# Layer 0 of a diffusion backbone: mean and Newton step of the inverse roots of queries and keys on GpSimd in place of VectorE

## The chip, the cores and the metric

One NeuronCore of a Trainium2 chip. It has a matrix engine (TensorE, PE below; its weight loads are PEld), VectorE (DVE), ScalarE (ACT), GpSimd (POOL) and SyncE (SP), which issues most DMAs. Each engine works through its own list of instructions in order, and waits on semaphores for the others. The metric is the device time of one execution in microseconds (us).

## The reference

Two layers of a backbone over 1024 latent tokens with a prefix of 256 context tokens, width 1024, float32. Layer 0 (the even layer) runs two kinds of grouped-query attention beside each other, each with 8 query heads and 2 key heads of width 64: [A] global, with RMSNorm of every query and key head and a rotary step, and [B] windowed, with a sink logit. Layer 1 runs a conformer convolution and a two-dimensional neighbourhood attention. The change lies in [A]'s RMSNorm:

```python
def rms_norm(x, g):
    xf = x.astype(jnp.float32)
    y = xf * lax.rsqrt(jnp.mean(xf * xf, axis=-1, keepdims=True) + EPS)
    return (y * g.astype(jnp.float32)).astype(x.dtype)
...
    def project(h):
        aq, ak, av, ag, bq, bk, bv, bg = split_cols(h @ w_in, EVEN_WIDTHS)
        aq = rms_norm(heads(aq, A_HEADS), q_gain)
        ak = rms_norm(heads(ak, A_KV_HEADS), k_gain)
...
    aq, ak, bq, bk = (apply_rope(t, cos, sin) for t in (aq, ak, bq, bk))
...
    y_lat = jnp.concatenate([oa * jax.nn.silu(ag), ob * jax.nn.silu(bg)], axis=-1) @ w_out
```

## The kernel before

The 1280 tokens are ten blocks of 128. Layer 0 treats four key heads `u` one after the other, in the order 2, 3, 0, 1: u = 2 and 3 are the windowed heads, u = 0 and 1 the global ones with the RMSNorm. A float32 matmul is made of three: every operand is split into a rounded part (on ACT, line 308: `hh`, `wh`, `hc`, `ph`) and a residual (on POOL or DVE, line 311: `hl`, `wl`, `hc`, `pl`), and PE multiplies high by high, low by high and high by low (lines 328 to 330).

Two strands are woven. The main one is attention for the head whose keys are ready, over blocks of 128 queries and chunks of 128 keys. It first finds upper bounds of the scores: PE computes them into the tile `mx` (lines 616, 628, 636), which has two banks, and DVE reduces them to `mp` (618, 629, 637 with a mask). DVE then makes the negated maximum `nmt` (412, or 415 to 422 with the sink), PE transposes it (`trn`, 433), and DVE puts it into `QL` (434), which enters the scores `st` (505, 509). ACT takes the exponent (`pf`, 517) and its rounded part `ph`; POOL subtracts to get the residual `pl` (in the blocks meant here DVE takes only every twelfth); PE multiplies by the values (`ov`, 456 to 461); DVE finishes the block (466 to 469, 666, 668).

The other strand fills in: it projects the next head (`proj_qkv`) and then its gate (`proj_gate`, product `pg`). `proj_qkv` makes five passes over pairs of token blocks. Each pass has two times 24 matmuls into the bank `pq`, which ACT copies to `pc` (three buffers, [128 tokens, 2 blocks, 5 heads of 64 and one of values]). For u = 0 and 1, and so ten times in all, the group of this change follows: ACT squares `pc` (line 844), DVE sums each head to `ss` (847, 128x10), makes the mean (848), POOL raises it to the power -0.5 (242, in `newton_rsqrt`), DVE refines it by one Newton step (243 to 245), and multiplies `pc` by the result `nr` (850) and by the gain (852). Then come the rotary products on DVE (861, 863) and their addition on POOL (865), and at last `qk_tail`: PE transposes the pair (`trk`, 873), ACT and DVE split it into `qs` and into the keys `KAt`, and SP writes `qs` to DRAM (876), from where attention loads it. Groups 0 to 4 below are those of u = 0 (305 to 370 us), groups 5 to 9 those of u = 1 (435 to 525 us). Lines 854 and 855 split the values into `Vt`. `newton_rsqrt` is called elsewhere too, from `rstd_steps` among others.

No order is written out by hand. A scheduler takes the program's instructions, simulates a timeline from its own cost estimates, and fixes each engine's list from it; priorities (`later`) and `issue_after` marks steer it. A changed instruction can thus shift the order of the instructions around it, on every engine.

## Time and profile before

| | |
|---|---|
| median of 3 runs | 1565.03 us (1564.26 to 1565.88) |
| the profiled execution | 1565.51 us, span 1563.7 us |
| mean granted TensorE clock | 0.963 |
| span in 21480 instructions: PE / DVE / ACT / POOL busy | 1465.1 / 1049.0 / 747.2 / 799.8 us |
| the ten powers (line 242, 128x10) on POOL | 19.6 us, 1963 ns each |

The span is the profiled time from the first to the last instruction. "Busy" leaves out waits, and a busy share averages over stages in which other engines set the pace. In a row of the timeline the first number is the start in us, the second the duration; then come engine, line, operation, output and inputs with their shapes, and in brackets how long the engine had been idle ahead of it and which instruction released it. A clock of 1.00 in a stretch means that PE ran at full speed there.

### The profile page before, as it was taken

To read this page: it belongs to the slowest core of one execution; us is meant where nothing else is said; L and a number is where in the kernel's file an instruction comes from. 1 tells how busy PE (TensorE), PEld (TensorE's weight loads), DVE (VectorE), ACT (ScalarE), POOL (GpSimd) and SP (SyncE) were. 2 spreads that over 40 slices of the span, in tenths; PEclk is the share of its full clock that TensorE was granted. 3 is DMA by queue.
4 is the path that set the end of the run, shared out by engine and by line. 5 is a ranking of instruction groups with operands and counts; after the bars stand their busy time and mean duration, and the time that the engine had idled before them with its cause. 6 is when DMAs were issued, how large, how long until landed. Compare 5 with 4: busy or idle time off the path is not lost.

```text
span 1563.7 us, 21480 instructions
## 1 busy us (share of the span) xinstructions
PE 1465.1 (94%) x7084; PEld 1174.2 (75%) x7084; DVE 1049.0 (67%) x2113; ACT 747.2 (48%) x1418; POOL 799.8 (51%) x637
## 2 busy tenths in 40 slices
PE   6899999998998999999999878999999999889995
PEld 2786887896896768876767557888887888667875
DVE  2832556589579765466677956999756466776766
ACT  3721434444435565447556663443334355554563
POOL 3430434455445766557646663665632244454665
PEclk7899999999999999999999989999999999889997
DMA  9473315422312245121112012111445788967632
GB/s 365 151 246 129 102 61 182 142 69 92 118 51 78 93 155 172 54 68 49 51 31 86 13 34 85 59 55 41 141 159 195 214 243 250 277 179 214 187 110 108
DMA packets 154168, 199.83 MB, mean 128 GB/s; under 512 B 14716, under 2 KB 95816, under 8 KB 154056
## 3 DMA queue, kind: packets, MB, share of 16 engines
q1 hardware_dynamic: 147392, 186.88, 38.0%
q10 hardware_dynamic: 6664, 11.57, 2.3%
q8 instruction: 56, 0.92, 0.3%
q14 instruction: 56, 0.46, 0.1%
HBM read 148.07 MB, written 49.02 MB: 126 GB/s over the span
## 4 chain that ended last, share of the span: by engine, by line
PE 73%; DVE 15%; DMA 4%; issue 3%; POOL 3%; ACT 2%; SPq 0%; DVEq 0%; ACTq 0%; POOLq 0%
PE p L328 6%; PE p L330 6%; PE p L329 6%; PE po L328 4%; PE po L329 4%; PE po L330 4%; PE ov L456 4%; PE ov L458 4%; PE ov L457 4%; PE st L505 3%; PE st L509 3%; PE pq L328 2%; PE pq L329 2%; PE pq L330 2%; PE pg L328 2%
## 5 line engine op out<-in xcount | busy, mean ns | idle before, releaser
L311 POOL TENSOR_TENSOR pl<-pf,ph 128x512 fp32r<-128x512 f32 (+4 forms) x321 | 394.8, 1241 | 359.7 <-ACT ph L308 305.8
L517 ACT ACTIVATE pf<-st 128x512 f32<-128x512 f32 x284 | 166.1, 596 | 204.3 <-PE st L509 164.3
L311 POOL TENSOR_TENSOR wl<-wr,wh 128x512 fp32r<-128x512 f32 (+2 forms) x131 | 170.5, 1314 | 164.6 <-ACT wh L308 137.7
L308 ACT CAST ph<-pf 128x512 fp32r<-128x512 f32 (+4 forms) x364 | 208.9, 587 | 26.9 <-PE ov L457 17.0
L328 PE MATMUL p<-hh,wh 128*128 128x512 f32 x448 | 178.0, 398 | 5.5 <-ACT hh L308 2.8
L329 PE MATMUL p<-hl,wh 128*128 128x512 f32 x448 | 176.2, 394 | 0.6 <-POOL hl L311 0.6
L330 PE MATMUL p<-hh,wl 128*128 128x512 f32 x448 | 173.8, 394 | 0.0
L456 PE MATMUL ov<-ph,Vt 128*128 128x512 f32 (+4 forms) x364 | 143.4, 394 | 8.3 <-DVE y L666 4.6
L505 PE MATMUL st<-QH,KAt 128*128 128x512 f32 (+4 forms) x364 | 141.4, 389 | 8.6 <-ACT pf L517 7.8
L458 PE MATMUL ov<-pl,Vt 128*128 128x512 f32 (+4 forms) x364 | 142.3, 391 | 2.0 <-POOL pl L311 1.9
L457 PE MATMUL ov<-ph,Vt 128*64 128x512 f32 (+4 forms) x364 | 140.4, 386 | 0.0
L509 PE MATMUL st<-QL,KBt 68*128 68x512 f32 (+4 forms) x364 | 136.0, 384 | 0.9 <-DVE QL L434 0.8
L1079 DVE SCALAR_TENSOR_TENSOR cps<-U,taps,cps 128x512 f32<-128x512 f32 x184 | 126.3, 748 | 0.9
L308 ACT CAST wh<-wr 128x512 fp32r<-128x512 f32 (+2 forms) x134 | 81.1, 613 | 91.8 <-DMA wr<-in_od_d_dram 19.9
L328 PEld LDWEIGHTS p<-hh,wh 128*128 128x128 f32 x448 | 85.3, 190 | 24.2 <-ACT hh L308 3.0
L329 PEld LDWEIGHTS p<-hl,wh 128*128 128x128 f32 x448 | 85.0, 190 | 19.1 <-POOL hl L311 1.7
L330 PEld LDWEIGHTS p<-hh,wl 128*128 128x128 f32 x448 | 85.1, 190 | 17.5
L629 DVE TENSOR_REDUCE mp<-mx 128x1 f32<-128x512 f32 x128 | 85.1, 680 | 17.8 <-PE mx L628 16.8
L328 PE MATMUL pq<-wh,hh 128*128 128x384 f32 x256 | 88.1, 344 | 2.8 <-ACT hh L308 2.8
L505 PEld LDWEIGHTS st<-QH,KAt 128*128 128x128 f32 x364 | 69.5, 191 | 27.5 <-ACT pf L517 12.1
L948 DVE SCALAR_TENSOR_TENSOR x<-po,modT,x 128x512 f32<-128x512 f32 (+1 forms) x72 | 47.0, 656 | 64.2 <-PE po L330 63.7
L456 PEld LDWEIGHTS ov<-ph,Vt 128*128 128x128 f32 x364 | 71.2, 196 | 24.9 <-ACT ph L308 5.2
(280 smaller groups left out, 3492.6 us busy)
## 6 DMA issues: line engine op xcount, KB each, us to landing
mw<-in_mod_w_dram SPq DMA_DIRECT2D x16, 1024.0 KB, 5.5
Q<-qs SPq DMA_DIRECT2D x40, 256.0 KB, 2.2
QH<-Q SPq DMA_DIRECT2D x80, 128.0 KB, 2.7
mw<-in_mod_w_dram SPq DMA_DIRECT2D x16, 512.0 KB, 6.5
wr<-in_od_d_dram SPq DMA_DIRECT2D x32, 256.0 KB, 3.1
wr<-in_ev_qkv_dram SPq DMA_DIRECT2D x16, 384.0 KB, 5.3
KAt<-KD SPq DMA_DIRECT2D x16, 384.0 KB, 6.2
wr<-in_od_wo_dram SPq DMA_DIRECT2D x22, 256.0 KB, 3.4
```

The source lines that it names most:

```text
L308: acts.append(SC.copy(hi, src))
L311: (GP if leng == "g" else VE).tensor_tensor(lo, src, hi.bitcast(F32), op=ALU.subtract)
L328: PE.matmul(o, lh, rh, start=first, stop=False)
L329: PE.matmul(o, lh, rl, start=False, stop=False)
L330: PE.matmul(o, ll, rh, start=False, stop=last)
L456: PE.matmul(o, V[:, 64:192], ph[:, :n], start=(t == 0), stop=False)
L457: PE.matmul(g.ov[0:64, q0 : q0 + n], V[:, 0:64], ph[:, :n], start=False, stop=False)
L458: PE.matmul(o, V[:, 64:192], pl[:, :n], start=False, stop=(last and g.sink is None))
L505: sts.append(PE.matmul(st[:, :n], KA[:, cs], g.QH[:, q0 : q0 + n], start=True, stop=False))
L509: PE.matmul(st[:, :n], KB[0:68, cs], g.QL[0:68, q0 : q0 + n], start=False, stop=True)
L517: acts.append(SC.activation(pf[:, :n], st[:, :n], AF.Exp, scale=1.0 if g.bias else SCALE))
L1079: VE.scalar_tensor_tensor(pc, uc, w, pc, op0=ALU.mult, op1=ALU.add)
```

## The change

In the groups of u = 0 and 1 the mean (848) and the three instructions of the Newton step, so far on DVE, become POOL instructions. The third DVE instruction form (a product with a constant folded in) is taken apart, so the Newton step has four instructions instead of three. DVE loses four instructions in each of ten groups; POOL has six where it had one. DVE hands `ss` over one instruction earlier and gets `nr` back finished.

```diff
--- before.py
+++ after.py
@@ -845,8 +845,14 @@
                     ss = ap.tile([P, 16], F32, tag="ss", name=nm("ss"), bufs=2)
                     s10 = ss[:, 0:10].rearrange("p (j h) -> p j h", j=2)
                     VE.tensor_reduce(s10, t2, axis=AX.X, op=ALU.add)
-                    VE.tensor_scalar(ss[:, 0:10], ss[:, 0:10], 1.0 / 64.0, EPS, op0=ALU.mult, op1=ALU.add)
-                    r = newton_rsqrt(ap, ss[:, 0:10], 10, "sr")
+                    GP.tensor_scalar(ss[:, 0:10], ss[:, 0:10], 1.0 / 64.0, EPS, op0=ALU.mult, op1=ALU.add)
+                    r = ap.tile([P, 16], F32, tag="srr", name=nm("nr"), bufs=2)
+                    t = ap.tile([P, 16], F32, tag="srt", name=nm("nt"), bufs=2)[:, 0:10]
+                    GP.tensor_tensor(r[:, 0:10], ss[:, 0:10], mhalf[:, 0:10], op=ALU.pow)
+                    GP.tensor_tensor(t, r[:, 0:10], r[:, 0:10], op=ALU.mult)
+                    GP.tensor_tensor(t, t, ss[:, 0:10], op=ALU.mult)
+                    GP.tensor_scalar(t, t, -0.5, 1.5, op0=ALU.mult, op1=ALU.add)
+                    GP.tensor_tensor(r[:, 0:10], r[:, 0:10], t, op=ALU.mult)
                     VE.tensor_tensor(p5, p5, r[:, 0:10].rearrange("p (j h) -> p j h", j=2)[:, :, :, None]
                                      .broadcast_to([P, 2, 5, 64]), op=ALU.mult)
                     VE.tensor_tensor(p5, p5, gain5[:, None, :, :].broadcast_to([P, 2, 5, 64]), op=ALU.mult)
```

From line 856 of the new kernel on, a line has a number higher by six: the product of `pc` and `nr`, 850 before, is 856, the gain 858, the addition on POOL 871. The number of instructions on PE, ACT and SP stays as it was but for a pair of rows on PE that are counted together. The scheduler's order is the same on all engines up to some 305 us, differs to about 850 us, is the same on PE from there to about 1350 us, and differs once more on PE and SP to about 1395 to 1420 us. In the rows below, a name's number is that of its buffer, and runs on differently in the two programs: `pc_3599`, `ss_3813`, `nr_3816` of before are `pc_3602`, `ss_3816`, `nr_3819` now (group 3), and `pc_5854`, `nr_6095` are `pc_5863`, `nr_6104` (group 9).

DVE in group 3, before (from the product of `pc` with `nr` to the sink block's `nmt`):

```order
L850 TENSOR_TENSOR pc_3599<-pc_3599,nr_3816 128x2x320
L637 ISA mx_2837,mp_2819<-mx_2837,k_bm 128x384
L637 ISA mp_2819 128x1
L852 TENSOR_TENSOR pc_3599<-pc_3599,gain_529 128x2x320
L861 TENSOR_TENSOR rt_852_3811<-pc_3599,k_cs 128x320 x2
L637 ISA mx_2852,mp_2819<-mx_2852,k_bm 128x384
L637 ISA mp_2819 128x1
L311 TENSOR_TENSOR qs_3887<-trk_3883,qs_3887 128x256
L863 TENSOR_TENSOR pc_3599<-pc_3599,k_cs 128x2x320
L415 TENSOR_REDUCE m_624_2856<-mp_2819 128x4
L311 TENSOR_TENSOR KAt_543<-trk_3883,KAt_543 64x128
L417 TENSOR_TENSOR nmt_2855<-m_624_2856,sink_155 128x4
```

DVE at the same place now:

```order
L637 ISA mx_2852,mp_2819<-mx_2852,k_bm 128x384
L637 ISA mp_2819 128x1
L311 TENSOR_TENSOR qs_3891<-trk_3887,qs_3891 128x256
L415 TENSOR_REDUCE m_624_2856<-mp_2819 128x4
L417 TENSOR_TENSOR nmt_2855<-m_624_2856,sink_155 128x4
L419 SCALAR_TENSOR_TENSOR se_2859<-nmt_2855,sink 128x4
L311 TENSOR_TENSOR KAt_543<-trk_3887,KAt_543 64x128
L421 CAST nmt_2855<-se_2859 128x4
L422 TENSOR_TENSOR nmt_2855<-se_2859,nmt_2855 128x4
L856 TENSOR_TENSOR pc_3602<-pc_3602,nr_3819 128x2x320
L466 STREAM_TRANSPOSE r_721_3263<-ov_3142 64x256 x2
L858 TENSOR_TENSOR pc_3602<-pc_3602,gain_529 128x2x320
```

The whole chain of `nmt` (415 to 422), which stood behind the products of `pc`, now stands ahead of them; the Newton step's three rows are gone.

POOL in group 3, before, from a split ahead of the power on:

```order
L311 TENSOR_TENSOR pl_2899<-pf_2900,ph_2898 128x512
L242 TENSOR_TENSOR nr_3816<-ss_3813,mhalf 128x10
L311 TENSOR_TENSOR pl_2919<-pf_2920,ph_2918 128x512
L311 TENSOR_TENSOR pl_3036<-pf_3037,ph_3035 128x512
L311 TENSOR_TENSOR wl_4005<-wr_4003,wh_4004 128x512
L311 TENSOR_TENSOR pl_3117<-pf_3118,ph_3116 128x512
L311 TENSOR_TENSOR wl_4011<-wr_4009,wh_4010 128x512
L865 TENSOR_TENSOR pc_3599<-pc_3599,rt_852_3811 128x2x320
```

POOL at the same place now:

```order
L848 TENSOR_SCALAR ss_3816<-ss_3816 128x10
L311 TENSOR_TENSOR pl_2919<-pf_2920,ph_2918 128x512
L851 TENSOR_TENSOR nr_3819<-ss_3816,mhalf 128x10
L311 TENSOR_TENSOR pl_3036<-pf_3037,ph_3035 128x512
L311 TENSOR_TENSOR pl_3117<-pf_3118,ph_3116 128x512
L852 TENSOR_TENSOR nt_3820<-nr_3819 128x10
L311 TENSOR_TENSOR wl_4010<-wr_4008,wh_4009 128x512
L853 TENSOR_TENSOR nt_3820<-nt_3820,ss_3816 128x10
L311 TENSOR_TENSOR wl_4016<-wr_4014,wh_4015 128x512
L854 TENSOR_SCALAR nt_3820<-nt_3820 128x10
L855 TENSOR_TENSOR nr_3819<-nr_3819,nt_3820 128x10
```

The six instructions of the group are not one behind the other: three `pl` and two `wl` stand between the mean and the last step.

DVE in group 9, before, behind row 243 of the Newton step:

```order
L244 SCALAR_TENSOR_TENSOR nt_6096<-nt_6096,nr_6095 128x10
L311 TENSOR_TENSOR qs_6084<-trk_6080,qs_6084 128x256
L629 TENSOR_REDUCE mp_4576<-mx_4615 128x1
L245 SCALAR_TENSOR_TENSOR nr_6095<-nt_6096,nr_6095 128x10
L629 TENSOR_REDUCE mp_4576<-mx_4634 128x1
L311 TENSOR_TENSOR KAt_546<-trk_6080,KAt_546 64x128
L850 TENSOR_TENSOR pc_5854<-pc_5854,nr_6095 128x2x320
L366 SCALAR_TENSOR_TENSOR sg_6281<-sg_6281,pg_6133 128x256
L629 TENSOR_REDUCE mp_4576<-mx_4637 128x1
L852 TENSOR_TENSOR pc_5854<-pc_5854,gain_529 128x2x320
L311 TENSOR_TENSOR qs_6289<-trk_6285,qs_6289 128x256
L412 TENSOR_REDUCE nmt_4640<-mp_4576 128x4
```

DVE at the same place now, to the first row that uses `nr`:

```order
L629 TENSOR_REDUCE mp_4581<-mx_4620 128x1
L311 TENSOR_TENSOR KAt_546<-trk_6089,KAt_546 64x128
L629 TENSOR_REDUCE mp_4581<-mx_4639 128x1
L366 SCALAR_TENSOR_TENSOR sg_6291<-sg_6291,pg_6143 128x256
L629 TENSOR_REDUCE mp_4581<-mx_4642 128x1
L311 TENSOR_TENSOR qs_6299<-trk_6295,qs_6299 128x256
L412 TENSOR_REDUCE nmt_4645<-mp_4581 128x4
L311 TENSOR_TENSOR KAt_546<-trk_6295,KAt_546 64x128
L366 SCALAR_TENSOR_TENSOR sg_6441<-sg_6441,pg_6315 128x256
L434 TENSOR_TENSOR QL_4568<-trn_4674,k_bd 4x512
L618 TENSOR_REDUCE mp_4744<-mx_4745 128x2
L856 TENSOR_TENSOR pc_5863<-pc_5863,nr_6104 128x2x320
```

The product of `pc` and `nr` went behind the `nmt` of that block, its `QL`, and the first reduction of the next block.

POOL in group 9, before, from the power to the addition:

```order
L242 TENSOR_TENSOR nr_6095<-ss_6092,mhalf 128x10
L311 TENSOR_TENSOR wl_6129<-wr_6127,wh_6128 128x512
L311 TENSOR_TENSOR pl_4676<-pf_4677,ph_4675 128x512
L311 TENSOR_TENSOR pl_4709<-pf_4710,ph_4708 128x512
L311 TENSOR_TENSOR pl_4763<-pf_4764,ph_4762 128x512
L311 TENSOR_TENSOR hc_7121<-hc_7121 128x512
L311 TENSOR_TENSOR pl_4803<-pf_4804,ph_4802 128x512
L311 TENSOR_TENSOR hc_7121<-hc_7121 128x512
L865 TENSOR_TENSOR pc_5854<-pc_5854,rt_1467_6090 128x2x320
```

POOL at the same place now; the last Newton step (855) comes next, and the addition (871) four rows behind these:

```order
L311 TENSOR_TENSOR wl_6139<-wr_6137,wh_6138 128x512
L311 TENSOR_TENSOR pl_4681<-pf_4682,ph_4680 128x512
L851 TENSOR_TENSOR nr_6104<-ss_6101,mhalf 128x10
L311 TENSOR_TENSOR pl_4714<-pf_4715,ph_4713 128x512
L311 TENSOR_TENSOR pl_4768<-pf_4769,ph_4767 128x512
L852 TENSOR_TENSOR nt_6105<-nr_6104 128x10
L311 TENSOR_TENSOR hc_7131<-hc_7131 128x512
L853 TENSOR_TENSOR nt_6105<-nt_6105,ss_6101 128x10
L311 TENSOR_TENSOR hc_7131<-hc_7131 128x512
L854 TENSOR_SCALAR nt_6105<-nt_6105 128x10
L311 TENSOR_TENSOR pl_4808<-pf_4809,ph_4807 128x512
L311 TENSOR_TENSOR pl_4849<-pf_4850,ph_4848 128x512
```

The `wl` that stood behind the power now stands ahead of it, and between the power and the last step there are six splits.

## The prediction, made before the run

> **What bounds the kernel now.** I began with the page: busy times and the chain that ended last.
>
> ```profile
> PE 1465.1 (94%) x7084; PEld 1174.2 (75%) x7084; DVE 1049.0 (67%) x2113; ACT 747.2 (48%) x1418; POOL 799.8 (51%) x637
> PE 73%; DVE 15%; DMA 4%; issue 3%; POOL 3%; ACT 2%; SPq 0%; DVEq 0%; ACTq 0%; POOLq 0%
> ```
>
> TensorE (PE) is busy for 94% of the span, so work taken off VectorE (DVE) counts only where PE waits for DVE. The ten groups that the change touches run in layer 0 between 305 and 525 us. The table by stages shows where DVE is full beside a PE that is not (columns: stretch, length, busy times, granted clock, DMA share, GB/s).
>
> ```profile
> 290.00:560.00 270.00, 258.54 (x1333) 218.41 (x1332) 207.58 (x456) 124.95 (x260) 148.49 (x108) 0.99 0.28 90
> 360.00:370.00 10.00, 7.73 (x46) 4.59 (x45) 9.00 (x19) 3.40 (x8) 4.76 (x5) 1.00 0.51 154
> 470.00:480.00 10.00, 7.37 (x34) 5.18 (x33) 9.22 (x22) 5.86 (x11) 6.50 (x5) 1.00 0.18 52
> 520.00:530.00 10.00, 7.68 (x26) 5.49 (x25) 9.75 (x15) 5.29 (x14) 7.04 (x7) 0.67 0.35 118
> 700.00:850.00 150.00, 141.37 (x620) 105.23 (x620) 101.22 (x187) 93.43 (x161) 92.61 (x72) 0.99 0.16 48
> ```
>
> Over the whole stage PE is idle for only 270 - 258.54 = 11.5 us, and most of that lies in three stretches in which DVE is 90 to 98% busy. The list of PE's waits from 290 to 560 us (total, times, longest) says who ends each wait:
>
> ```profile
> PE trk L873 <- DVE KAt L311: 1.9, 2, 1.4
> PE trn L433 <- DVE nmt L422: 1.8, 2, 1.3
> PE mx L628 <- DVE mp L629: 1.7, 3, 1.0
> PE ov L458 <- POOL pl L311: 1.2, 1, 1.2
> PE mx L636 <- DVE mp L618: 1.0, 1, 1.0
> ...
> PE st L505 <- ACT pf L517: 0.9, 1, 0.9
> PE pg L330 <- POOL wl L311: 0.8, 1, 0.8
> ```
>
> DVE ends 1.9 + 1.8 + 1.7 + 1.0 = 6.4 us of it, GpSimd (POOL) 2.0. So the most that can be won from waits is about 11 us of 1565, and POOL, to which the work goes, already ends a part of them.
>
> **What is removed, and what is added.** The groups by shape, 300 to 540 us (columns: count | busy us, mean ns | idle before, releaser), and three small POOL groups of the whole run:
>
> ```profile
> L243 DVE TENSOR_TENSOR nt<-nr,ss 128x10 f32<-128x10 f32 x10 | 6.0, 599 | 5.3 <-POOL nr L242 5.3
> L244 DVE SCALAR_TENSOR_TENSOR nt<-nt,nr 128x10 f32<-128x10 f32 x10 | 5.9, 590 | 0.2
> L245 DVE SCALAR_TENSOR_TENSOR nr<-nt,nr 128x10 f32<-128x10 f32 x10 | 3.1, 309 | 0.2
> L848 DVE TENSOR_SCALAR ss<-ss 128x10 f32<-128x10 f32 x10 | 2.2, 220 | 0.1
> L242 POOL TENSOR_TENSOR nr<-ss,mhalf 128x10 f32<-128x10 f32 x10 | 19.6, 1963 | 18.1 <-DVE ss L848 9.0 <-PE mx L616 6.3 <-DVE nmt L422 2.5
> L311 POOL TENSOR_TENSOR pl<-pf,ph 128x512 fp32r<-128x512 f32 x54 | 72.3, 1351 | 49.5 <-ACT ph L308 40.5 <-PE ov L457 3.2 <-PE ov L458 3.2
> L855 POOL TENSOR_TENSOR Vt<-pc,Vt 128x128 fp32r<-128x128 f32 x10 | 4.9, 496 | 8.3 <-ACT Vt L854 7.2 <-PE trn L433 1.0
> L1050 POOL MEMSET U<- 128x15 f32 x4 | 0.4, 112 | 0.0
> ```
>
> DVE loses 40 instructions, 6.0 + 5.9 + 3.1 + 2.2 = 17.2 us, and the 5.3 us that it stood waiting for the power. POOL keeps the power (1963 ns) and gains 50 instructions of 128x10. No row shows a multiplication of that size on POOL. From below the 128x15 memset bounds it at 0.11 us, from above the 128x128 Vt at 0.50. Between the 512-wide pl (1.351) and Vt (0.496) the slope is 0.855 / 384 = 2.2 ns an element, so Vt without its width costs 0.496 - 128 x 0.0022 = 0.21 us. I take that, nearer the memset, since neither has a width to speak of: 50 x 0.21 = 10.5 us (5.5 to 25). POOL is busy for 148.5 of 270 us here, so its sum has room; what counts is where the instructions stand.
>
> The chain of one group in itself grows little: DVE's 0.16 to 1.26 us for each of three steps become 0.2 each on POOL, and the crossings stay two (sum of squares to POOL, inverse root back). The spread on DVE is itself telling:
>
> ```profile
> 322.19 0.16 DVE L243 TENSOR_TENSOR nt<-nr,ss 128x10 f32<-128x10 f32 x1
> ...
> 350.92 1.26 DVE L243 TENSOR_TENSOR nt<-nr,ss 128x10 f32<-128x10 f32 x1 [0.57 <-POOL nr L242]
> ```
>
> The same instruction takes 0.16 us alone and 1.26 where POOL began a pl just ahead of it. The removed steps were therefore mostly waiting behind POOL's splits, and on POOL they stand in one row with these instead. The scheduler's new order puts up to six splits between a group's POOL steps, so in groups 0, 3, 6 and 9 the inverse root comes later than before, by the 1.35 us of each split. That has a price only where something urgent stands behind the pc product on DVE. No DMA is added or moved by the edit itself; Qd's writes follow the tails and shift with them by a few us, and in the second layer's start a KAt load and a QH load pass three smaller ones on SyncE's queue.
>
> **Place A, group 3 (347 to 367 us).** Before, the pc chain of group 3 stands ahead of the sink block's nmt chain on DVE:
>
> ```profile
> 353.66 1.90 DVE L850 TENSOR_TENSOR pc<-pc,nr 128x640 f32<-128x640 f32 x1
> 360.04 0.81 DVE L863 TENSOR_TENSOR pc<-pc,k_cs 128x640 f32<-128x640 f32 x1
> 348.92 1.96 POOL L242 TENSOR_TENSOR nr<-ss,mhalf 128x10 f32<-128x10 f32 x1
> 361.27 1.27 DVE L417 TENSOR_TENSOR nmt<-m,sink 128x4 fp32r<-128x4 f32 x1
> 364.47 0.28 PE L433 MATMUL trn<-ident,nmt 128*12 128x128 f32 x1 [1.32 <-DVE nmt L422]
> ```
>
> Now all of L415 to L422 stands ahead of the pc product. The chain of pc from 353.66 to 360.85, 7.2 us with a few rows between, goes behind it, so nmt ends before PE gets to trn (364.47 - 1.32 = 363.15): -1.3 us. On POOL the steps of group 3 are spread over pl, pl, pl, wl, wl. From 348.92 on, five splits, the power and five steps (5 x 1.35 + 1.96 + 1.05 = 9.8) give the inverse root at some 358.7 us, or 360 if a split waits for its input, which is about when DVE is done with nmt. DVE may stand there for 0 to 3 us, with QL of the next block behind it. Taken 0, the nearer end.
>
> **Place B, groups 8 and 9 (515 to 533 us).**
>
> ```profile
> 520.15 1.23 DVE L243 TENSOR_TENSOR nt<-nr,ss 128x10 f32<-128x10 f32 x1 [0.42 <-POOL nr L242]
> 518.16 1.96 POOL L242 TENSOR_TENSOR nr<-ss,mhalf 128x10 f32<-128x10 f32 x1
> 520.09 1.26 POOL L311 TENSOR_TENSOR wl<-wr,wh 128x512 fp32r<-128x512 f32 x1
> 521.41 0.39 PE L330 MATMUL pg<-hc,wl 128*128 128x256 f32 x1 [0.80 <-POOL wl L311]
> 523.61 0.80 PE L628 MATMUL mx<-KAt,QH 128*128 128x512 f32 x1 [1.02 <-DVE mp L629]
> 524.91 0.87 PE L873 MATMUL trk<-ident,pc 128*128 128x128 f32 x3 [0.50 <-DVE KAt L311]
> 526.01 0.63 PE L456 MATMUL ov<-ph,Vt 128*128 128x512 f32 x1
> 530.27 0.41 PE L328 MATMUL pg<-hh,wh 128*128 128x512 f32 x1
> 532.62 0.39 PE L329 MATMUL pg<-hl,wh 128*128 128x512 f32 x1
> ```
>
> Three waits follow each other: 0.80 + 1.02 + 0.50 = 2.3 us. Behind them the granted clock falls (0.67 in the stretch): ten starts take 526.01 to 530.27, 0.426 us each, against ten in 530.27 to 532.62, 0.235. That is 4.26 - 2.35 = 1.9 us more. In the new order wl stands ahead of the power, L243 to L245 are gone from between the maxes, and pc x nr of group 9 stands behind the nmt, QL and first maxes of the next block. I take all of it as won: -4.2 us (0 to -4.2; none if another wait keeps PE idle as long). That the slow clock goes with the waits is argued from their order alone: at 470 to 480 us PE was idle for 2.6 us and the clock stayed at 1.00. [...]
>
> Two debts stand against it. Group 9's last four steps now have six splits between them, so the rotated pc comes some 2 us later, and a pl that stands right behind its addition comes later with it: 0 to +3, taken +1.0, the lower part, since pl mostly waits for ACT (40.5 of 49.5 us of POOL's idle ahead of it). At place C (groups 6 and 7, 445 to 480 us) the steps of group 6 have splits between them too:
>
> ```profile
> 453.75 1.87 DVE L850 TENSOR_TENSOR pc<-pc,nr 128x640 f32<-128x640 f32 x1
> ```
>
> By the same count as at A the inverse root comes some 1.5 us after that 453.75; the stretch of 470 to 480 has 2.6 us of PE idle, which the fewer DVE rows shorten and the later pc lengthens: -1 to +2.5, taken +0.5.
>
> Elsewhere the order differs up to 850 us and again about 1350 to 1395 us. 700 to 850 has 150 - 141.37 = 8.6 us of PE idle that can move either way; I price these at 0, +-2.5.
>
> **The sum.** -1.3 - 4.2 + 1.0 + 0.5 = -4.0 us on the profiled execution's 1565.51 (span 1563.7 and 1.8 around it), hence 1561.5; the median of the three runs is 0.5 below that execution, so 1561.0. The bounds of the terms add up to -1.3 - 4.2 + 0 - 1 - 2.5 = -9.0 and, with nothing won at B, to -1.3 + 3 + 0 + 3 + 2.5 + 2.5 = +9.7. They hardly fall together; half of the way from the sum to each gives this case's own range, -6.5 to +2.9, or 1558.5 to 1567.9.
>
> **The rivals.**
> 1. The waits move on. DVE, over 90% busy at 470 to 480 and at 520 to 530, stays above 75% there without a group's 17.2 / 10 = 1.7 us; the next reduction, a KAt or a pl ends PE's wait in place of the old one, and the slow clock comes with it. Then -1.3 at A, 0 at B, and the debts of +1.5 make about 0: 1565. For it: at 470 to 480 us the engines take turns in ending the waits. Against it: at B all three rows are ones that the new order loosens.
> 2. Slower, by POOL's queue. Groups 0, 3, 6 and 9 have their steps between splits; DVE, in its fixed order, stands at the pc product with QL (A) or reductions (C) behind it, and there are two banks for mx, so PE stands with it. It decides if the inverse root comes over 2 us later than the row ahead of the product is done. Two such groups at 2 to 3 us of PE's time, with nothing won at A or B, give +4 to +6 on 1565.0: 1569 to 1571. For it: 1.35 us for each split, and 5.3 us that DVE already waited for the power alone. Against it: what stands behind the product is in most groups the product's own chain.
> [...]
>
> **How the numbers follow.** Forecast 0.45, waits move on 0.30, POOL's queue 0.18, the port 0.07. No change that can be told is within 0.2%, 3.1 us. Of the forecast's share three quarters lie past -3.1 us (its sum is near that bound) and the rest within; add some 0.07 of the second case, where the reorder behind 560 us helps: faster 0.41. Rivals 2 and 3 give nearly all of slower: 0.24. The rest, 0.35, is the same. The range leaves out a tenth at each end: 1555.5, 3 us below the forecast case's own range, where the 2.6 us of idle at 470 to 480 go too, to 1570, the middle of rival 2.
>
> **What would show it.** [...] PE's wait of 1.3 us at trn near 364 and the three near 521 to 525 are gone, and 520 to 530 shows a clock near 1.00. DVE's waits for nr of 2 us and more at L856 mean rival 2. The prediction is wrong if PE's idle time from 290 to 560 us is not 3 us or more below 11.5, or if the stretch from 560 to 850, or that after 1350, changes by more than 2.5 us.

## The result, and the profile after

The changed kernel takes 1569.04 us (median of 11 runs, 1566.42 to 1571.95), the kernel before 1564.26 on the same chip (11 runs, 1559.71 to 1568.40). The ratio is 1.0036 with a 95% interval of 1.0022 to 1.0051: slower, by about 5 us, where 4 us less had been forecast. The profiled execution of the changed kernel took 1569.36 us (span 1567.5), which is 3.8 us of span above the profiled execution of before.

First the busy line of the page after:

```profile
PE 1467.7 (94%) x7084; PEld 1178.2 (75%) x7084; DVE 1026.3 (65%) x2073; ACT 749.3 (48%) x1418; POOL 809.8 (52%) x687
```

The work did move: DVE has 40 instructions and 22.7 us less (17.2 of them the removed rows), POOL 50 more and 10.0 us more. PE runs as many matmuls as before and is busy for 2.6 us more, most of the 3.8 us of span, so the same matmuls took longer in some places. The answer lies in single stages. I cut both traces at the same transposes `trn` (line 433), which end the blocks of 128 queries. The columns are stretch, length, busy time and count of PE, PEld, DVE, ACT and POOL, granted clock, DMA share, GB/s. Before:

```profile
0.00:340.25 340.25, 317.19 (x1638) 248.81 (x1639) 180.06 (x427) 134.57 (x287) 131.06 (x109) 0.95 0.48 164
340.25:394.53 54.28, 49.84 (x261) 40.32 (x260) 48.19 (x98) 25.54 (x56) 30.81 (x22) 1.00 0.29 92
445.60:506.00 60.40, 55.70 (x279) 45.77 (x278) 52.87 (x125) 26.60 (x56) 31.68 (x25) 1.00 0.23 69
506.00:534.50 28.50, 26.18 (x137) 21.73 (x134) 25.69 (x40) 14.01 (x33) 20.85 (x16) 0.88 0.28 93
575.20:633.00 57.80, 54.04 (x259) 42.78 (x258) 33.33 (x58) 29.92 (x50) 38.53 (x28) 1.00 0.54 181
633.00:1563.70 930.70, 870.36 (x4063) 697.70 (x4061) 657.63 (x1255) 470.99 (x854) 499.36 (x406) 0.96 0.40 122
```

After:

```profile
0.00:338.19 338.19, 312.49 (x1639) 246.49 (x1640) 175.52 (x414) 134.66 (x287) 134.00 (x124) 0.97 0.49 165
338.19:395.70 57.51, 52.43 (x262) 42.54 (x261) 45.49 (x92) 24.05 (x54) 31.66 (x31) 0.91 0.27 87
446.80:514.00 67.20, 62.18 (x284) 50.37 (x282) 48.90 (x116) 27.07 (x56) 33.35 (x36) 0.90 0.21 62
514.00:536.70 22.70, 22.70 (x134) 19.75 (x133) 15.98 (x28) 14.14 (x32) 19.52 (x23) 1.00 0.35 117
577.20:638.10 60.90, 54.86 (x248) 43.13 (x247) 31.38 (x57) 30.58 (x51) 37.98 (x28) 0.92 0.52 166
638.10:1567.50 929.40, 871.40 (x4074) 699.22 (x4072) 653.58 (x1256) 472.82 (x854) 500.04 (x407) 0.96 0.40 122
```

(The two stages left out, 394.5 to 445.6 and 534.5 to 575.2 us, differ by 0.0 and 0.2 us.) The differences are -2.1, +3.2, +6.8, -5.8, +3.1 and -1.3; with 0.0 and -0.2 they make the 3.8. What the reader is to see is the column of the clock. In each of the three stages that grew it fell from 1.00 to between 0.90 and 0.92, and in the stage that shrank by 5.8 us it rose from 0.88 to 1.00. In the stage from 340 us PE ran 261 and 262 matmuls; idle time grew by (57.51 - 52.43) - (54.28 - 49.84) = 0.6 us, busy time by 2.6. So more of the loss is matmuls at half clock than waits. In the other stages the counts differ (5 matmuls more from 446 us, 3 fewer from 514, 11 fewer from 577 and 11 more behind 638 us), since the new order moves a few across the marks; at the 0.235 us from start to start of the ten matmuls from 530.27 to 532.62 us in before, 11 of them are some 2.6 us, an estimate. The gain of 2.1 us at the start is complete at 301 us (a `trn` at 301.28 us before, at 299.21 after), and the two orders are the same up to some 305 us; it goes with the clock (0.95 against 0.97) and not with the change.

PE's waits from 290 to 560 us in the changed kernel (total, times, longest):

```profile
PE trn L433 <- DVE nmt L422: 3.0, 1, 3.0
PE ov L456 <- DVE y L666: 2.7, 2, 1.9
PE trk L879 <- DVE KAt L311: 2.1, 1, 2.1
```

The transposes that waited twice for 1.3 us and less now wait once, for 3.0. And the moved rows, in groups (count | busy us, mean ns | idle before, releaser):

```profile
L851 POOL TENSOR_TENSOR nr<-ss,mhalf 128x10 f32<-128x10 f32 x10 | 19.6, 1962 | 0.7
L848 POOL TENSOR_SCALAR ss<-ss 128x10 f32<-128x10 f32 x10 | 2.4, 237 | 11.3 <-DVE ss L847 10.8
L855 POOL TENSOR_TENSOR nr<-nr,nt 128x10 f32<-128x10 f32 x10 | 2.1, 206 | 0.8
L856 DVE TENSOR_TENSOR pc<-pc,nr 128x640 f32<-128x640 f32 x10 | 9.7, 974 | 6.1 <-POOL nr L855 6.1
```

A step of 128x10 other than the power costs POOL 0.20 to 0.24 us in the mean, as estimated (0.21). DVE waits for the finished inverse root for 6.1 us in ten groups, hardly more than the 5.3 it waited for the power, but 2.66 us of that is one wait, in group 7:

```profile
468.66 0.83 DVE L856 TENSOR_TENSOR pc<-pc,nr 128x640 f32<-128x640 f32 x1 [2.66 <-POOL nr L855]
```

**Where the new wait comes from.** The rows at 357 to 383 us in the changed kernel (start, duration; idle before and releaser in brackets), from DVE, POOL and PE:

```profile
357.27 0.82 DVE L856 TENSOR_TENSOR pc<-pc,nr 128x640 f32<-128x640 f32 x1 [1.68 <-POOL nr L855]
373.14 1.89 DVE L856 TENSOR_TENSOR pc<-pc,nr 128x640 f32<-128x640 f32 x1 [1.19 <-POOL nr L855]
375.07 1.80 DVE L858 TENSOR_TENSOR pc<-pc,gain 128x640 f32<-128x640 f32 x1
380.11 1.52 DVE L419 SCALAR_TENSOR_TENSOR se<-nmt,sink 128x4 f32<-128x4 f32 x1
```
```profile
373.07 4.94 POOL L311 TENSOR_TENSOR pl<-pf,ph 128x512 fp32r<-128x512 f32 x3
```
```profile
379.29 0.52 PE L879 MATMUL trk<-ident,pc 128*128 128x128 f32 x3 [2.08 <-DVE KAt L311]
383.28 0.38 PE L433 MATMUL trn<-ident,nmt 128*12 128x128 f32 x1 [3.00 <-DVE nmt L422]
```

In group 3 the `nmt` chain now goes first, as forecast, and PE's wait near 364 us is gone. But the `pc` chain of group 3 starts later, and that of group 4, behind it, waits 1.19 us for POOL's last step and then runs beside three splits on POOL (4.94 us), where its two products take 1.89 and 1.80 us. The next block's `nmt` stands behind them, and PE waits 2.08 and 3.00 us at 377 to 383. The wait has moved on by one block of queries.

**What the wait does to the clock.** Stretches of 3.4 us ahead of a fall and the fall itself, after:

```profile
377.70:381.10 3.40, 0.99 (x5) 0.58 (x5) 3.30 (x7) 0.63 (x2) 1.33 (x2) 1.00 0.20 77
381.10:391.30 10.20, 8.02 (x26) 6.87 (x27) 9.58 (x22) 3.66 (x9) 3.02 (x3) 0.50 0.33 106
473.20:476.70 3.50, 2.04 (x8) 1.24 (x7) 3.50 (x8) 2.60 (x6) 1.36 (x2) 0.99 0.00 0
579.10:582.50 3.40, 2.21 (x7) 1.17 (x7) 3.32 (x8) 0.69 (x2) 3.40 (x3) 0.99 0.70 211
582.50:592.60 10.10, 6.16 (x16) 4.58 (x17) 4.48 (x8) 4.31 (x7) 7.22 (x5) 0.50 0.89 289
```

And before:

```profile
363.00:366.40 3.40, 2.08 (x18) 0.89 (x18) 2.95 (x8) 1.39 (x4) 2.31 (x3) 1.00 0.46 133
380.10:383.50 3.40, 1.83 (x9) 0.99 (x8) 3.27 (x8) 0.98 (x3) 3.40 (x3) 1.00 0.46 154
520.00:523.40 3.40, 1.79 (x11) 1.16 (x9) 3.21 (x4) 0.49 (x3) 3.40 (x4) 1.00 0.00 0
523.40:530.20 6.80, 6.09 (x15) 4.51 (x16) 6.74 (x12) 4.97 (x12) 3.84 (x4) 0.50 0.52 174
```

In the clock's own records of both traces the granted clock falls to 0.50 for 3.41 us or a multiple of it (10.24 is three; only the last record of each, 14.34 and 18.28 us, is no multiple, and runs past the end of the span), and all its changes lie on one grid of 3.41 us. PE was busy for 0.99 of 3.40 us ahead of the fall at 381 (29%), 2.04 of 3.50 at 476 (58%), 2.21 at 582 (65%), and before for 1.79 at 523 (53%). Before, the stretches at 363 (61%) and 380 (54%) went without one. Cut at this grid, from 100 to 1500 us, the traces of before and after hold 774 stretches that began at full clock: with PE busy below 50% all of 11 were followed by half clock, from 50 to 70% 9 of 29, from 70 to 80% 3 of 23, above that none of 711. Over ten traces of this case I counted 72 of 76, 28 of 108, 15 of 121 and none of 3577. So the kernel before stood at 363 and 380 in a band in which some stretches were followed by half clock and others not.

**A knock-on behind the groups.** At 575 to 633 us nothing of the change runs any more, but the order on SyncE's queue is another. After, SP, ACT and PE:

```profile
573.22 0.37 SPq L933 DMA_DIRECT2D hl<-Od  x1
573.71 1.24 SPq L603 DMA_DIRECT2D QH<-Q  x2
576.62 0.42 SPq L933 DMA_DIRECT2D hl<-Od  x1
```
```profile
584.83 1.04 ACT L308 CAST hh<-hl 128x1024 fp32r<-128x1024 f32 x1 [5.00 <-DMA x<-in_xT_dram]
```
```profile
586.44 0.58 PE L328 MATMUL po<-hc,wh 128*128 128x256 f32 x1 [4.10 <-ACT wh L308]
```

Before, the two loads of `hl` stood one behind the other (572.77 to 574.0 us, two rows in one entry). Now loads of queries and a write come between them, the second is issued at 576.62 and lands 8.2 us later, ACT's rounding waits 5.00 us for it (the releaser shown is another transfer, long done by its own row), the rounding of `wh` stands behind it on ACT, and PE waits 4.10 us, from 582.34 on. The fall of the clock at 582.5 comes as this wait begins: in the stretch ahead of it (579.1 to 582.5, above) PE was 65% busy, because of shorter waits. The clock then stays half for 10.1 us, 3.9 of them inside the long wait.

### The profile page after: what moved, and what is told of

It is laid out like the page before. It is cut to its first block, busy times and chain, and to the rows that moved or that the text cites. A ratio compares the mean times of both kernels' runs of the same rounds, so it can differ in the third digit from the quotient of the medians.

```text
span 1567.5 us, 21482 instructions
## 1 busy us (share of the span) xinstructions
PE 1467.7 (94%) x7084; PEld 1178.2 (75%) x7084; DVE 1026.3 (65%) x2073; ACT 749.3 (48%) x1418; POOL 809.8 (52%) x687
## 5 line engine op out<-in xcount | busy, mean ns | idle before, releaser
L505 PEld LDWEIGHTS st<-QH,KAt 128*128 128x128 f32 x364 | 70.3, 193 | 29.3 <-ACT pf L517 11.4
```

The costliest lines, as they stand in the source:

```text
L505: sts.append(PE.matmul(st[:, :n], KA[:, cs], g.QH[:, q0 : q0 + n], start=True, stop=False))
```

## The experiments

Each was timed beside runs of the kernel before on its own chip; ratios are to those runs, with 95% intervals. The first four shared one chip, the next four another, the last four a third.

**Half of the groups.** In the first two kernels the new lines stand under `if u == 0:` or `if u == 1:`, and the old two lines under `else:`. The third leaves the Newton step out and has the mean on DVE, so the power alone is POOL's, as before:

```diff
-                    GP.tensor_scalar(ss[:, 0:10], ss[:, 0:10], 1.0 / 64.0, EPS, ...)
+                    VE.tensor_scalar(ss[:, 0:10], ss[:, 0:10], 1.0 / 64.0, EPS, ...)
...
                     GP.tensor_tensor(r[:, 0:10], ss[:, 0:10], mhalf[:, 0:10], op=ALU.pow)
-                    GP.tensor_tensor(t, r[:, 0:10], r[:, 0:10], op=ALU.mult)
-                    GP.tensor_tensor(t, t, ss[:, 0:10], op=ALU.mult)
-                    GP.tensor_scalar(t, t, -0.5, 1.5, op0=ALU.mult, op1=ALU.add)
-                    GP.tensor_tensor(r[:, 0:10], r[:, 0:10], t, op=ALU.mult)
```

The fourth is the changed kernel once more.

> The move in groups 0 to 4 (u = 0) alone; groups 5 to 9 as before. Theory 1 (clock): the change gathers PE's short waits into the same few microseconds, and the granted clock halves behind them. Then this kernel keeps the new stall of about 5 us at 377 to 383 us with some 10 us at half clock behind it, has the old one at 521 to 525 us too, and is 3 us slower than before (about +0.2%). Theory 2 (late inverse root): DVE stands at the product for nr, and PE behind it; then slower by the 3 us of waits for nr in these groups even where the clock stays full. Theory 3 (the scheduler's order behind 575 us is to blame): within 1 us of before, if the order there is the old one.

> The move in groups 5 to 9 (u = 1) alone; groups 0 to 4 as before. Theory 1 (clock): half clock at 476 to 500 us costs some 6 us in a run whose windows fall badly, the gain of 5.7 us at 506 to 535 us is kept: between -3 and +3 us, with a wide spread. Theory 2 (late inverse root): +2 us, from the waits for nr in groups 6 and 9. Theory 3 (order behind 575 us): +3 us, all of it between 575 and 633 us.

> Leaves the Newton step out altogether in all ten groups: mean on DVE and power on POOL as before, no multiplication behind it on either engine. DVE has 30 instructions (15 us) fewer than before and POOL has none more. Theory 2 (late inverse root on POOL): the loss is gone, and DVE's freed time shows as a gain: 3 to 5 us faster than before. Theory 1 (clock): PE's waits stay near 10 us in the stage of 340 to 580 us, because another wait takes the place of each, and the time follows the half clock: within 4 us of before, either way. Theory 3: as the move itself, +3 to +5 us, if the order behind 575 us is the moved kernel's.

> The moved kernel once more, for a second profile of the same program. Theory 1 (clock): the waits of PE come back at the same places to 0.2 us, but the stretches at half clock do not all come back, because they depend on where the 3.4 us windows fall; a profile with fewer of them is shorter by about half of what is missing. Theory 2 and 3: waits and time come back alike, and the half clock explains nothing of the 4.8 us.

| kernel | median us (runs) | ratio | mean granted clock |
|---|---|---|---|
| groups 0 to 4 moved | 1571.35 (6) | 1.0062 (1.0046 to 1.0078) | 0.960 |
| groups 5 to 9 moved | 1563.14 (12) | 1.0016 (1.0001 to 1.0031) | 0.964 |
| no Newton step at all | 1569.09 (6) | 1.0054 (1.0038 to 1.0071) | 0.963 |
| the changed kernel again | 1570.21 (7) | 1.0053 (1.0034 to 1.0072) | 0.958 |
| before | 1560.76 (18) | | 0.966 |

The stage from 340 us, with groups 0 to 4 moved and then with groups 5 to 9:

```profile
339.10:396.60 57.50, 52.42 (x263) 42.55 (x261) 45.29 (x92) 24.05 (x54) 31.68 (x31) 0.91 0.28 88
```
```profile
338.30:392.60 54.30, 49.86 (x262) 40.29 (x260) 48.23 (x98) 25.54 (x56) 30.78 (x22) 1.00 0.28 92
```

The loss at 340 us comes with groups 0 to 4 alone (57.5 against 54.3 us). Groups 0 to 4 alone are no better than the whole change: they keep this loss, and the stage at 506 us keeps 27.8 us in place of 22.7. Every theory had this kernel at most 3 us slower than before, and it was 10.6 us slower by the medians; its profile is 2.1 us behind that of before at the `trn` near 635 us and loses 3.6 more behind it, with 91.7 us at half clock there against 77.7. What brings that about behind 635 us was not looked for. Groups 5 to 9 alone cost 2.4 us; the theories had -3 to +3.

The third kernel was a miss for all three theories (3 to 5 us faster, within 4 us, 3 to 5 us slower): it was 8.3 us slower by the medians, as slow as the changed one. Its stage at 340 us takes 55.9 us without a fall of the clock, but holds 290 matmuls against 261, so the lengths can't be compared, and the profiled execution was the fastest of its six. Where the loss lies stays open. Its mean clock is 0.003 below that of before, which is 9 us more at half clock in 1565 us. In before, ten matmuls took 4.26 us at half clock against 2.35, so by an estimate from these about half of the 9 us is lost at most, and the falls of the clock are only a part of it. Nor did it save the time that was left out: DVE has 30 rows fewer, 15.0 us of work, but is busy for 1043.9 us against 1049.0; other rows grew, the ten products of `pc` with `nr` from 11.4 to 14.4 us and those with the gain from 8.8 to 13.3. Fewer rows on an engine that waits and is waited for do not make this kernel faster by themselves.

In the repeat the falls of the clock at 381 and 578 us recur (10.2 us each), that at 445 to 514 only in part (3.4 of 13.7). The stage there is 2.8 us shorter than in the first profile, at the same order, but still 4.0 longer than before:

```profile
446.30:510.70 64.40, 58.54 (x284) 47.49 (x282) 49.91 (x116) 26.86 (x56) 33.38 (x36) 0.97 0.21 65
```

In the kernel with the new order and the old engines, below, it is 65.4 us with 6.8 us at half clock. So about half of the 6.8 us lost there goes with the falls, and about half stays with the order; the two were not taken apart by a run.

**Engine and order apart.** A local edit moves the scheduler's order everywhere, so two kernels were pinned. After the program is built, each engine's instructions are chained along a table of places taken from the other kernel's list:

```diff
         tile_kernel(tc, args, out)
+        pin(nc, tc)
...
+    for e, text in ORD.items():
+        at, last = -1, None
+        for step in text.split():
+            at += int(step)
+            i = by[e][at]
+            if last is not None:
+                tc.add_manual_dep(i, last.name, DependencyInfo(NoSync, DATA), reason="pin")
+            last = i
```

One has the moved steps in the order of before; the other has DVE's old steps in the changed kernel's order. A third put useless matmuls ahead of the transpose that waits 3.00 us, the fourth was before once more; both of these had one run and a profile.

> The move in all ten groups, but every engine's list is pinned to the order of the kernel before: PE, ACT and SP have exactly the old lists, DVE's list only lacks the 40 moved rows, and on POOL the six steps stand one behind the other where the power stood. Theory O (order): the loss came with the new order, not with the work on another engine; in the old order the move wins DVE's time at 380 to 385 and 521 to 525 us and loses nothing: 1 to 4 us faster than before. Theory P (POOL): the steps on POOL deliver the inverse root late and hold up the splits behind them; then it stays 3 to 6 us slower than before in the old order too.

> The other half: mean and Newton step stay on DVE as before (mean right behind the sum of squares, Newton step right ahead of the product), but every engine's list is pinned to the order of the moved kernel. Theory O (order): it is slower than before by as much as the moved kernel or more, +4 to +8 us, with the 5 us of waits at 377 to 383, the wait for wh at 580 us and the half clock behind both. Theory P (POOL): without the POOL steps the loss is gone, within 1 us of before.

> The moved kernel with 12 useless matmuls of 512 columns (0.235 us each) behind the last product of the block that ends at 380 us, ahead of trn: PE does 2.8 us more work, all of it in the 3.0 us in which it would wait for nmt; behind this block the scheduler's order differs somewhat. Theory C (the clock goes by how busy PE was in fixed windows of 3.4 us, and the 10 us at half clock behind 381 us cost 4 us): the stretch at half clock gets shorter by 3.4 to 10.2 us, and the time from the trn at 359 us to the one at 396 is 1.5 to 4 us shorter in spite of the added work. If the clock does not hang on PE's idle time: that time is the same or up to 1 us longer, and 10.2 us at half clock stay.

> The kernel before once more, for a second profile. Every theory: the same waits. Theory C: full clock from 340 to 520 us again, since no window there falls much under 0.55 busy, and half clock behind the waits at 521 to 525 us, unless these fall into two windows.

| kernel | median us (runs) | ratio | mean granted clock |
|---|---|---|---|
| moved steps, old order | 1566.01 (12) | 1.0032 (1.0018 to 1.0047) | 0.962 |
| old engines, new order | 1569.34 (6) | 1.0057 (1.0042 to 1.0071) | 0.958 |
| before | 1560.53 (17) | | 0.967 |

The new order without the moved steps costs as much as the change, so POOL's added work and its queue are not needed for the loss. Its waits at 338 to 396 us:

```profile
PE trn L433 <- DVE nmt L422: 3.0, 1, 3.0
PE trk L873 <- DVE KAt L311: 1.4, 1, 1.4
```

Its product in group 7 starts where the changed kernel's does (468.66), without the long wait for POOL, and PE's waits from 447 to 512 us are those of the repeat, to 0.1 us:

```profile
468.60 0.82 DVE L850 TENSOR_TENSOR pc<-pc,nr 128x640 f32<-128x640 f32 x1
```

The moved steps in the old order were slower too, by 5.5 us, where theory O had them 1 to 4 us faster and theory P 3 to 6 slower. DVE waits for `nr` there for 6.5 us, 2.59 and 2.37 at the longest, so a late inverse root from POOL does come with the steps in this order. The stage at 340 us, and its falls of the clock:

```profile
339.35:397.77 58.42, 54.54 (x262) 43.39 (x261) 46.80 (x93) 25.13 (x56) 32.68 (x32) 0.91 0.27 86
361.40:364.70 3.30, 3.30 (x9) 1.53 (x10) 2.93 (x5) 0.91 (x4) 2.30 (x2) 0.50 0.37 121
385.30:392.00 6.70, 6.69 (x17) 5.34 (x18) 6.01 (x14) 2.91 (x6) 2.52 (x2) 0.50 0.23 80
```

PE is idle for 58.42 - 54.54 = 3.9 us, less than the 4.4 of before, and the stage is still 4.1 us longer: its busy time grew by 4.7 us for the same matmuls, all of it in two falls of the clock. Here PE's idle time got shorter and the stage longer. That kernel's stage at 506 us takes 28.2 us with 6.8 at half clock, as before, so the gain of 5.8 us there comes with the new order and not with the engine.

The third kernel, with 12 useless matmuls, took 38.1 us for the block from 359.5 where the changed kernel took 37.2 from 358.5; 1.5 to 4 us less had been expected. Its stretch at half clock shrank from 10.2 to 3.4 us, but the useless matmuls themselves ran in it:

```profile
381.40:384.70 3.30, 3.30 (x10) 0.93 (x8) 3.16 (x8) 0.75 (x3) 1.16 (x1) 0.50 0.37 122
```

The 3.4 us ahead of the fall are those of 377.7 to 381.1 in the changed kernel, and the first of these matmuls starts at 381.06, so this filler came 3.4 us too late.

The second profile of before has full clock from 340 to 520 us again and 3.4 us at half clock at 525, as expected.

**The waits filled.** If the falls of the clock are the loss, useless matmuls inside the waits must win it back, at no other change. Each engine's order was pinned, and the matmuls (a square of the identity into a bank that is overwritten next) set at fixed places:

```diff
+        for at, n in FILLS.get((kind, no), ()):
+            for _ in range(n):
+                f = PE.matmul(t, identr, identr[:, None, :].broadcast_to([P, 4, P]), start=True, stop=True)
```

In the moved steps with the old order 5 stand near 360 and 6 near 382 us; the same eleven in before are the control. In the changed kernel in its own order 20 fill the waits at 377 to 383 us and 16 the wait of 4.10 us at 582. The last kernel is before with 61 in its longest waits.

> As moved_old_order (the move in the old order on every engine), with 11 useless matmuls of 512 columns put into PE's list and nothing else changed: 5 ahead of the pm product at 360 us and 6 ahead of the trk transposes at 382, where PE waits 1.6 and 1.4 us. Theory C (the clock halves behind a window of 3.4 us in which PE was busy for about half): no half clock at 361 and 385 us, the time from the trn at 339 us to the one at 398 falls from 58.4 to some 54 us, and the whole is 3 to 5 us faster than moved_old_order, within 1.5 us of the kernel before, though PE has 2.6 us more to do. If the move costs by POOL or DVE: the same 58 us or 1 to 2 more.

> The control: the kernel before in its own order, with the same 11 matmuls at the same two places, where its waits are 0.9 and 1.4 us. Theory C: no half clock stood there, so nothing is to be won: the segment stays at 54.3 us or is 0.3 longer, the whole within 1 us of before. If filling helps by something else than the clock: faster by 2 us or more here too.

> The moved kernel in its own order, pinned, with 36 useless matmuls: 8 and 12 in the two waits of 2.1 and 3.0 us at 377 to 383 us, 16 in the wait of 4.1 us for wh at 582 us. PE has 8.5 us more to do, all of it in waits. Theory C: the stretches at half clock behind 381 and 582 us (10.2 us each) go, the segment from 338 to 396 us falls from 57.4 to 53.5 us, that from 577 to 638 from 60.7 to 57.5, and the whole is 6 to 8 us faster than the moved kernel, at or 1 us below the kernel before. If the clock is no cause: 0 to 3 us slower than the moved kernel.

> A version that the theory points to: the kernel before in its own order, with useless matmuls in the longest of its own waits: 6 ahead of pq at 56 us, 6 ahead of trk at 382, 11 ahead of po at 745, 14 ahead of po at 928, 11 ahead of p at 960, 7 ahead of p at 1205, 6 ahead of trn at 1361 us (61 of 0.235 us, 14 us of added work). Theory C: the stretches at half clock behind 747, 931, 962 and 1208 us go (6.8, 6.8, 6.8 and 3.4 us, half of each lost), and part of that behind 1361: 8 to 14 us faster than before, 0.5 to 0.9%. If the clock is no cause: 0 to 2 us slower.

| kernel | median us (runs) | ratio | mean granted clock |
|---|---|---|---|
| moved steps, old order, 11 | 1564.03 (12) | 1.0020 (1.0004 to 1.0036) | 0.964 |
| before, the same 11 | 1562.05 (12) | 1.0008 (0.9995 to 1.0021) | 0.965 |
| changed, own order, 36 | 1563.23 (12) | 1.0010 (0.9997 to 1.0023) | 0.965 |
| before, 61 | 1561.77 (12) | 1.0006 (0.9993 to 1.0019) | 0.973 |
| before | 1561.12 (35) | | 0.966 |

The changed kernel with 36 matmuls more than it needs is at 1.0010, where without them it was at 1.0053 and 1.0036 (on other chips, each against its own runs of before). Its interval does not touch that of the repeat (1.0034 to 1.0072), and overlaps by 0.0001 with the first. That is 4 to 7 us won back, where 6 to 8 had been expected. The control gained nothing (1.0008), so here the filler did not help where there was no fall. The two filled stages of the changed kernel:

```profile
340.26:394.31 54.05, 53.54 (x281) 43.25 (x280) 44.57 (x92) 24.02 (x54) 31.99 (x31) 1.00 0.29 93
576.30:636.00 59.70, 56.77 (x265) 45.27 (x264) 31.92 (x57) 30.78 (x51) 37.92 (x28) 0.97 0.52 169
```

57.51 became 54.05 us, with the clock at 1.00 and 20 useless matmuls more to run, and 60.90 became 59.70, where 3.4 us at half clock were left. This execution was the slowest of its twelve (1565.99 us): the falls from 446 to 514 us came in full (13.6 us), and other places had more than in the changed kernel, so the stages can be read from it and the whole cannot. In the old order the filled stage takes 55.5 in place of 58.4 us without a fall, against 54.3 before, so 2.9 of the 4.1 us lost there go with the falls. The interval of the whole kernel still overlaps that of its unfilled twin (1.0018 to 1.0047): for that pair the stage shows it and the time does not, where 3 to 5 us had been expected.

The control shows one thing more. At 506 us, where its lists are those of the kernel before, its profile has no fall of the clock, and the stage takes 26.0 us in place of 28.5:

```profile
505.86:531.86 26.00, 23.35 (x135) 19.79 (x134) 24.90 (x38) 14.06 (x32) 18.71 (x15) 1.00 0.30 96
```

Filling before itself was a miss, with 8 to 14 us less expected: the 899 to 1234 us stretch got its clock back and little time. Before, and with 61 matmuls:

```profile
899.30:1234.60 335.30, 319.96 (x1457) 261.57 (x1456) 243.42 (x398) 140.51 (x233) 165.74 (x126) 0.96 0.34 108
```
```profile
897.50:1230.50 333.00, 322.20 (x1489) 262.64 (x1488) 243.24 (x398) 140.48 (x233) 165.97 (x126) 0.99 0.34 109
```

Half clock went from 23.9 to 6.8 us and the stretch from 335.3 to 333.0 us; the whole kernel did not gain. That the fillers reached past the end of some waits and so cost what the clock gave is how I read the busy time (up by 2.2 us in spite of the faster clock), but it was not tried with fewer of them. No version beat the kernel before.

## Why the prediction was wrong, step by step

- **What leaves DVE and what POOL pays: right.** 40 rows and 17.2 us gone; 0.20 to 0.24 us a step on POOL against 0.21 estimated. No run shows the term behind the third rival's chance of 0.07, "the port", which is also a part of the 0.24 for slower. What the rows show instead: the power aside, POOL's longest single step took 0.53 us; and of DVE's 40 small rows in before, the nine that began up to 0.3 us behind the start of a 512-wide split on POOL took 1.11 to 1.27 us, those without a POOL row beside them 0.13 to 0.17.
- **Place A, -1.3 us: the wait went, the term was wrong.** The wait at 364 us is gone. The stage still took 3.2 us more, because the `pc` chains of groups 3 and 4 ran later and the same wait came back 19 us on, longer, with 10.2 us at half clock behind it. With these waits filled the stage is back at 54.05 us, so the clock is what they cost. The order showed those chains behind `nmt`; the prediction followed the one row that got earlier and not the next block's `nmt` behind the rows that got later.
- **Place B, -4.2 us: right there, and partly by luck.** The three waits and the half clock behind them are gone: 28.5 to 22.7 us. But 2.5 of these 5.8 us are the fall of the clock, which the control was spared as well with nothing changed there. The prediction took 1.9 us for it, from ten matmuls that started in 4.26 of the 6.8 us. It also put the fall behind three waits: it starts at 523.5 us, behind two of them (0.80 and 1.02 us), and the third runs in it at half clock already. The debt of +1.0 behind group 9 did not come: the product waits 0.53 us for `nr`, and the stage that follows is 0.2 us shorter.
- **Place C, +0.5 (-1 to +2.5): wrong.** It took 6.8 us more, with two falls of the clock (0.90). The late inverse root was that of group 7 and not of group 6. B and C together went from 88.9 to 89.9 us, and in the repeat to 87.1, where 3.7 us less had been forecast. With 6.8 us at half clock the old order takes 88.9 us there and the new order with old engines 89.0, with 3.4 us the second profile of before 88.0 and the repeat 87.1: at an equal clock the new order wins 0 to 1 us at B and C.
- **Elsewhere, 0 +-2.5: wrong at 575 us**, where the order on SyncE's queue cost 3.1 us through a wait of 4.10 and 10.1 us at half clock; the filled kernel got 1.2 us of that back. Behind 633 us the stage is 1.3 us shorter, within the 2.5.
- **The step that failed** is that the clock was a term at B only. There the prediction took the 1.9 us of half clock as won along with the waits; everywhere else it counted waits in PE's idle time alone. Summed waits from 290 to 560 us did not grow (10.1 us after from the stage rows, 5.1 + 5.0, against 11.5; the test of 3 us less failed). What grew is the time at half clock in the stages from 340 to 633 us: about 34 us of it (10.2 + 13.7 + 10.2) against 6.8. Read from the stages with fewer falls, it was worth some 3 us at A, some 3 at C and 1 at 575 us, more than the 5.5 us that were to be won. Over the whole of the two profiles the half clock grew by less, from 115.2 to 121.5 us, since other places happened to have fewer falls. The mean clock of the repeat's runs, 0.958 against 0.966, comes to 25 us more of it in 1565 us.
- **Rival 1** (the waits move on) was right on the waits, and gave 1565 since it let the clock come with them in the old place only. **Rival 2** (POOL's queue) gave a time, 1569 to 1571, that came true, and its sign came once: the wait of 2.66 us for `nr` in group 7. But the kernel with the same order and none of POOL's new work starts that product at the same time and is as slow, so the time came by another way. In the old order, with waits of 2.59 and 2.37 us, rival 2 has a part. The measured time lies in the stated range only because the range reached up to the middle of this rival; the forecast case's own range ended at 1567.9.
- **What the rows of before had already shown.** At 520 us two waits, of 0.80 and 1.02 us, left PE busy for 1.79 of 3.40 us, 1.6 us of idling, and half clock followed at 523.4. What the prediction did not draw from it is that every cluster of short waits is then a candidate: 9 of the 29 stretches with PE busy for 50 to 70% in the traces of before and after were followed by half clock.

Shown: the order alone costs as much as the change; the steps alone, in the old order, cost 0.2 to 0.5%; filling two places with useless work takes most of the loss back. Over the runs of before the time falls with the mean granted clock as well, by 0.34, 0.55 and 0.75 us for each 0.001 on the three chips (correlations -0.25, -0.55 and -0.71). From 0.966 to 0.958, before and the repeat, that would be 3 to 6 of the 8 to 9 us measured there; an estimate, since a correlation within a kernel is not a cause. It does not hold from one kernel to another: before with 61 useless matmuls has a clock of 0.973 and no less time, and the kernel without a Newton step is 8 us slower at 0.963.

Open: the falls at place C were not filled, so their part is read from four executions of the same order alone; what makes the kernel without the Newton step slow, and groups 0 to 4 alone behind 635 us; and whether the moved steps leave a cost of their own of about 0.1% in the old order, which the intervals of the last runs can't tell from none.

## What to carry to other kernels

Where PE is the bound, don't price a reordering by idle time alone: for each cluster of waits take PE's busy share over some 3.4 us before and after. In the two traces here all 11 stretches below one half and 9 of 29 from there to 70% were followed by half clock, and at A, where the share was 29%, the 10.2 us at half clock were worth some 3 us. Before crediting an edit to its engine, pin the old order and move the work, then pin the new order and leave the work: here each half was slower by itself. And follow a moved row one block further than the wait it removes, to the rows that now stand behind it.

## What the hardware showed that was not expected

- In the traces of before and after the clock fell behind all 11 stretches of 3.4 us in which PE was busy for less than half, and at 523.4 us in before behind one of 53%, in which no single wait was longer than 1.02 us. Between 50 and 70% it did in 9 of 29, and the same kernel differed in one stage by 2.8 us from one execution to another (67.2 and 64.4 us, with 13.7 and 3.4 us at half clock).
- The clock came back in steps of 3.41 us (records of 3.41, 6.83 and 10.24 us), also where PE was fully busy at half speed through the whole stretch (3.30 of 3.30 us at 361.4).
- A useless matmul can pay: 36 of them, 0.235 us each by an estimate from the ten starts at full clock in before, brought the changed kernel from 1.0036 and 1.0053 to 1.0010, and 61 in the kernel before, at its own longest waits, won nothing.
